# Weights' hi and lo parts kept in DRAM by the first block, and a recurrence's transfers on GpSimd's queue

## The chip, the cores and the metric

One core of one Trainium2 chip runs the kernel. The metric is the device time of an execution in microseconds; the lower is the better.

## The reference

It is one layer of a decoder trunk over 16 meta tokens and a sequence of 2048, with 1024 channels, in float32:

```python
u = rms_norm(h, norm_mix_g)
proj = u @ w_in + b_in
y_attn = sliding_window_sink_attention(q, k, v, sinks)
y_rwkv = rwkv7_time_mix(p_rwkv, ...)
merged = gates[..., :D] * (y_attn @ w_br_attn) + gates[..., D:] * (y_rwkv @ w_br_rwkv)
h = h + merged @ w_o
f = rms_norm(h, norm_ffn_g)
h = h + (silu(f @ w_ffn_gate) * (f @ w_ffn_up)) @ w_ffn_down
return rms_norm(h, norm_final_g)[:, 16:]
```

The attention looks back 128 positions in 8 heads (2 for keys and values) with rotary positions and a sink. The other mixer is RWKV-7, a recurrence with a state of 64x64 for each of 8 heads. The products of weights are a 1024 x 4640 input projection, two of 512 x 1024, one of 1024 x 1024, and three of 1024 x 2816.

## The kernel before, in words

**Precision.** A product with a weight is made of three matmuls on TensorE in the type fp32r: hi times hi, hi times lo and lo times hi, where hi is the rounded value and lo what rounding leaves. `mm3` (line 221) emits the three. Weights and activations are both split so.

**Weights.** They come in chunks of 128 x 1024 floats (512 KB). A chunk is eight weight tiles of 128 x 128. `chunk` (line 208) loads one into `wraw` (two buffers) on SP's queue, writes the hi part with ACT and the lo part with DVE into tiles of the tag `wsp` (five buffers, so two chunks and a half). All this has high priority: the framework's planner, which fixes each engine's order of instructions from a simulated timeline, puts it as early as buffers allow. Each of the four blocks loads and splits the same 119 chunks again: 37 of `w_in`, 8 of `w_br`, 8 of `w_o`, 22 each of gate, up and down.

**Blocks and phases.** The sequence is cut into four blocks of 512 positions. First `phase_a` (line 353) runs for all four blocks: norm, input projection, and its outputs to DRAM (`proj_d`, `gate_d`). Then `phase_c` (line 440) runs for all four: branch products, gates, output projection, FFN, final norm. `add_to_h` (line 377) adds the products of `w_o` and `w_down` to the residual.

**Mixers.** Attention (`attn`, line 914, 16 tiles of 128 positions) and recurrence (`rwkv`, line 606, 32 units of 256 positions and one pair of heads, and one unit for the meta tokens) are generators. The driver (line 1060 on) advances them by `tick` while the phases emit dense work, a step for some microseconds of it. TensorE's instructions run in the order in which they are emitted (`InOrder`, whose calls all have line 93); the queues of the other engines are ordered by the planner and then run strictly in order.

**One unit of the recurrence.** After its elementwise work on ACT and DVE, a product `g` is made (line 739). Four transfers on SP write it to `lt_d` in DRAM (line 744), one reads it back as `lt`, spread over the partitions (line 754), and one loads the start value `xv` (line 757); `xv` and `lt` have one buffer each. GpSimd then inverts triangular blocks in 31 steps of a product `pr` and a sum into `xv` (lines 761, 763) and writes the result to `xt_d` on its own queue (line 788). Some ticks later four transfers on SP read it as `td` (line 793; one buffer, which the unit before still reads until its last step). DVE transposes a part of it into `tq` (line 797), TensorE forms `pq` from that, and the four steps of the recurrence follow: `ch` on TensorE, copies `rd`, `sf`, `yt` on ACT, `ud` and the state `sd` on DVE. The output's norm has a power on GpSimd (line 850), and `yf` goes to `y_d` on SP (line 861), from where `phase_c` loads it (`Ys`, line 405).

**What else is on GpSimd:** the rotary positions of attention (`q`, `kl`, `kr`, lines 883 to 885 and 934 to 936), the power in each norm (line 232), a part of the final scaling (line 526).

**What else is on SP:** the loads of x, of the projections for the mixers, of y and the gates, and a part of the output. A line 202 in the rows is any call of high priority on ACT or DVE, 212 is the load of a weight.

Of the kernel before, what the change touches and what calls it, by code (L numbers as in the profile page):

```python
# [19 lines left out]
F32 = mybir.dt.float32  # L20
# [7 lines left out]
P = 128  # L28
# [50 lines left out]
def layer(ctx, tc, x, meta, w_in, w_br, w_o, w_gate, w_up, w_down, w2a, a2, g2, vecs, sinks, gfin,  # L79
# [124 lines left out]

    HA, HV = High(A), High(V)


    def chunk(src, name, pin=False):

        with tc.high_priority():  # L210
            raw = dn.tile([P, D], F32, tag="wraw", bufs=2, name=f"wr_{name}")
            r = S.dma_start(raw, src)
            if name == "in_0_%d" % ORDER[0]:
                late(r)
        hi, lo = (dn.tile([P, D], F32R, tag="wsp", bufs=5, name=f"w{q}_{name}") for q in "hl")
        made = HA.activation(hi, raw, AF.Copy), HV.tensor_sub(lo, raw, f32(hi))
        if pin:
            late(made[0]), late(made[1])
        return hi, lo

# [132 lines left out]
    def phase_a(b):  # L353
        u = nxt[0] or rows_of(b)
        nxt[0] = None
        rest = None
        ws = []
        mid = lambda ci: lambda: ws.append(chunk(w_in[ci], f"in_{b}_{ci}", True))
        for n_, ci in enumerate(ORDER):
            w = ws.pop(0) if ws else chunk(w_in[ci], f"in_{b}_{ci}")  # L360
            if ci == ORDER[20] and b < NB - 1:
                nxt[0] = rows_of(b + 1)
            if ci == ORDER[-1] and b == NB - 1:
                nxt[0] = Ys(0)
            yield from in_chunk(b, ci, u, w, nxt[0] if ci == ORDER[-1] else None, mid(ORDER[n_ + 1]) if b == 0 and n_ < 2 else None)
            if rest:
                rest()
                rest = None
            if b == 0 and ci == ORDER[0]:
                load_rest()  # L370
                meta_norm()
            if b == 0 and ci in META_CH:
                rest = meta_chunk(ci, w)
            else:
                emitted[b].add(ci)

    def add_to_h(h, ms, src, name, last=None):

# [3 lines left out]
        def part(t, hf):  # L382
            if hf not in ws:
                ws[hf] = chunk(src[hf], f"{name}_{hf}")
            w = ws[hf]
# [54 lines left out]
    def phase_c(b):  # L440
# [6 lines left out]
        for f in range(KT):  # L447
            tg = []
            for q in range(2):
                g_ = dn.tile([P, 512], F32, tag="ld", bufs=4, name=f"tg_{b}_{f}_{q}")  # L450
                S.dma_start(g_, gate_d[8 * q + f][:, tk])
                tg.append(g_)
            w = chunk(w_br[f], f"br_{b}_{f}")
            y[0]
# [14 lines left out]
            if len(grp) == 4:  # L469
                yield from add_to_h(h, grp[:2], w_o[f // 2 - 1], f"o{b}_{f}")  # L470
                grp = grp[2:]
        rows, st = [], []

        def normed(t, hf):
# [3 lines left out]
            if hf:  # L478
# [8 lines left out]

        yield from add_to_h(h, grp, w_o[KT // 2 - 1], f"o{b}_l", normed)
        grp = []
        yield NORM_US  # L490
        fz = Acts(rows, "g_ffn", f"f{b}")
        ws = [chunk(w_gate[0], f"g_{b}_0")]

        mids = [lambda: ws.append(chunk(w_up[0], f"u_{b}_0", True)),
                lambda: ws.append(chunk(w_gate[1], f"g_{b}_1", True))]
        for n in range(NFF):
            pss = []
            for nm, src in (("g", w_gate), ("u", w_up)):
                w = ws.pop(0) if ws else chunk(src[n], f"{nm}_{b}_{n}")
                ps = psd.tile([P, 512], F32, tag="pd", name=f"p{nm}_{b}_{n}")  # L500
                yield from product(ps, w, fz, mid=mids.pop(0) if mids else None)
                pss.append(ps)
            th = dn.tile([P, 512], F32, tag="tmp", bufs=2, name=f"th_{b}_{n}")
            HA.activation(th, pss[0], AF.Tanh, scale=0.5)
            HV.scalar_tensor_tensor(th, th, 1.0, pss[0], op0=ALU.add, op1=ALU.mult)
            HV.tensor_mul(th, th, pss[1])
            grp.append(split_of(th, f"g{b}_{n}"))
            if len(grp) == 4:
                yield from add_to_h(h, grp[:2], w_down[n // 2 - 1], f"d{b}_{n}")
                grp = grp[2:]  # L510
# [19 lines left out]

        yield from add_to_h(h, grp, w_down[NFF // 2 - 1], f"d{b}_l", finished)

# [73 lines left out]
    def rwkv(i, j):  # L606
# [125 lines left out]
        for x in range(2):  # L732
# [5 lines left out]
            if x == 0:  # L738
                V.tensor_mul(g[:, :, 0], pv[:, :, 0], rnb.unsqueeze(2).to_broadcast([P, n, CH]))
                for h in range(2):  # L740
                    for q in range(2):
                        r32, o = slice(64 * h + 32 * q, 64 * h + 32 * q + 32), slice(32 * q, 32 * q + 32)
                        m0 = (2 * q + h) * 4
                        S.dma_start(lt_d[uid, m0:m0 + n].rearrange("c j i -> j c i"), g[r32, :, 0, o])
                V.tensor_mul(g[:, :, 1], pv[:, :, 1], cc("gincl").unsqueeze(1).to_broadcast([P, n, CH]))
            else:
# [6 lines left out]
        lt = mx.tile([P, 32, 32], F32, tag="lt", bufs=1, name=f"lt_{nm}")  # L753
        S.dma_start(lt.rearrange("p j i -> p (j i)"),
                    lt_d[uid].rearrange("m j i -> m (j i)").unsqueeze(0).to_broadcast([8, 16, 1024]))
        xv = mx.tile([P, 4, 32], F32, tag="xv", bufs=1, name=f"xv_{nm}")
        S.dma_start(xv.rearrange("p c i -> p (c i)"), consts[:, slice(*_CC["x0"])])
        for r in range(31):
# [31 lines left out]
        for h in range(2):  # L790
            for q, r32 in ((0, lo[h]), (1, hi[h])):
                m0 = (2 * q + h) * 4
                S.dma_start(td[r32, :, r32], xt_d[uid, m0:m0 + 4].rearrange("m j i -> j m i"))
        yield
# [65 lines left out]
        V.tensor_mul(yf, yf, gs)  # L860
        S.dma_start(y_d[4 + j][:, i * TU:(i + 1) * TU], yf)

# [315 lines left out]
```

## Time and profile before

| what | value |
|---|---|
| median of 3 runs | 3419.69 us (3419.29 to 3424.39) |
| the profiled execution | 3412.06 us |
| its span, first to last instruction | 3410.3 us |
| TensorE, matmuls | 3263.3 us busy, 96% |
| DVE | 1929.6 us, 57% |
| ACT | 1499.4 us, 44% |
| GpSimd (POOL) | 1004.8 us, 29% |
| mean granted TensorE clock | 0.984 |
| DMA | 409.50 MB, 120 GB/s on average |

PE is TensorE's matmuls, PEld its loads of weights into the array, which run beside them. Busy time counts instructions of the engine; time in which it waits or issues a transfer is not busy, but on GpSimd the issue of a transfer is listed as work. A row of waits says which instruction sat idle, what ended the wait, and how long this was in total, how often, and at most. A row of the timeline is: start, duration, engine, line, operation, output and inputs, and in brackets the idle time before it with what ended it. The granted clock is 1.00 at 2.4 GHz and 0.50 at 1.2 GHz.

### The profile page before, as it was taken

How to read it: one execution, taken by the hardware profiler on the slowest of the kernel's cores; microseconds unless marked ns; L12 is line 12 of the kernel's file. 1: busy time of each engine (PE TensorE's matmuls, PEld its weight loads, DVE VectorE, ACT ScalarE, POOL GpSimd, SP SyncE). 2: the span in 40 equal slices, each digit the busy share in tenths (PEclk: the TensorE clock that was granted, in tenths of full speed). 3: DMA queues.
4: the chain of work that ended last, by engine and by line, in shares of the span. 5: the costliest groups of instructions: out<-in, count | busy, mean ns of one | idle time of the engine just before them, and what ended most of it. 6: DMA issues, size and time to landing. Idle time of an engine off the chain costs nothing.

```text
span 3410.3 us, 47506 instructions
## 1 busy us (share of the span) xinstructions
PE 3263.3 (96%) x16909; PEld 2682.7 (79%) x16909; DVE 1929.6 (57%) x3860; ACT 1499.4 (44%) x3101; POOL 1004.8 (29%) x2290
## 2 busy tenths in 40 slices
PE   8999999999999989999989899999989999999999
PEld 6887778887778777778868788887777888778887
DVE  3344445554544775656667656657655555764455
ACT  4455456554544564445443533434353333432222
POOL 0133333343333343333343244334333341100000
PEclk9999999999999999999989999999999999999999
DMA  4544444454544433333244333335332332522222
GB/s 144 160 144 129 161 133 134 140 157 133 163 131 139 142 103 103 97 91 102 85 139 151 95 102 101 90 98 168 122 95 85 102 94 90 196 96 94 98 99 99
DMA packets 227027, 409.50 MB, mean 120 GB/s; under 512 B 61829, under 2 KB 120581, under 8 KB 226790
## 3 DMA queue, kind: packets, MB, share of 16 engines
q1 hardware_dynamic: 192854, 356.98, 34.5%
q10 hardware_dynamic: 32352, 47.31, 4.0%
q8 instruction: 133, 2.18, 0.3%
q0 software_dynamic: 1584, 2.18, 0.2%
q14 instruction: 104, 0.85, 0.1%
HBM read 346.29 MB, written 60.04 MB: 119 GB/s over the span
## 4 chain that ended last, share of the span: by engine, by line
PE 46%; issue 20%; POOL 20%; DMA 7%; DVE 4%; ACT 2%; SPq 1%; POOLq 0%; ACTq 0%; DVEq 0%
PE pi L93 15%; POOL pr L761 9%; POOL xv L763 8%; PE pg L93 7%; PE pu L93 7%; PE ph_d L93 5%; PE ch L93 2%; PE pb L93 1%; PE ph_o L93 1%; PE py L93 1%; DMA lt<-lt_d 1%; DMA wr_in<-in_w_in 1%; DMA xt_d<-xv 1%; DVE h L202 1%; PE ph_d_l L93 1%
## 5 line engine op out<-in xcount | busy, mean ns | idle before, releaser
L93 PE MATMUL pi<-act_u,wh_in 128*128 128x512 f32 x2368 | 764.1, 404 | 2.3 <-DVE act_u L202 2.1
L761 POOL TENSOR_TENSOR pr<-xv,lt 128x124 f32<-128x124 f32 (+30 forms) x992 | 398.1, 401 | 584.6 <-DMA lt<-lt_d 468.9
L93 PEld LDWEIGHTS pi<-act_u,wh_in 128*128 128x128 f32 x2368 | 425.3, 190 | 83.2 <-issue 5.7
L93 PE MATMUL pi<-act_u,wl_in 128*128 128x512 f32 x1184 | 465.6, 393 | 0.6 <-DVE wl_in L202 0.6
L93 PE MATMUL pg<-act_f,wh_g 128*128 128x512 f32 x1408 | 453.6, 403 | 7.2 <-DVE act_f L202 7.1
L93 PE MATMUL pu<-act_f,wh_u 128*128 128x512 f32 x1408 | 446.7, 398 | 0.0
L93 PE MATMUL ph_d<-wh_d,mg_g 128*128 128x512 f32 x1280 | 428.4, 399 | 16.4 <-DVE th L202 13.6
L763 POOL TENSOR_TENSOR xv<-xv,pr 128x124 f32<-128x124 f32 (+30 forms) x992 | 380.9, 384 | 76.5
L93 PEld LDWEIGHTS pg<-act_f,wh_g 128*128 128x128 f32 x1408 | 256.5, 190 | 57.5 <-DVE act_f L202 9.8
L93 PEld LDWEIGHTS pu<-act_f,wh_u 128*128 128x128 f32 x1408 | 257.5, 189 | 50.3 <-issue 1.5
L93 PEld LDWEIGHTS ph_d<-wh_d,mg_g 128*128 128x128 f32 x1280 | 241.7, 189 | 69.8 <-DVE th L202 15.2
L202 DVE TENSOR_TENSOR wl_in<-wr_in,wh_in 128x1024 fp32r<-128x1024 f32 x148 | 187.0, 1264 | 184.4 <-PE pi L93 126.8
L93 PE MATMUL pg<-act_f,wl_g 128*128 128x512 f32 x704 | 277.6, 394 | 0.0
L93 PE MATMUL pu<-act_f,wl_u 128*128 128x512 f32 x704 | 275.8, 392 | 0.0
L93 PEld LDWEIGHTS pi<-act_u,wl_in 128*128 128x128 f32 x1184 | 223.4, 189 | 51.0 <-DVE wl_in L202 1.0
L93 PE MATMUL ph_d<-wl_d,mg_g 128*128 128x512 f32 x640 | 250.4, 391 | 0.0
L850 POOL TENSOR_TENSOR gst<-gst,mhalf 128x4 f32<-128x4 f32 x32 | 36.1, 1128 | 707.2 <-DVE gst L849 656.8
L202 DVE SCALAR_TENSOR_TENSOR h<-ph_d,h 128x512 f32<-128x512 f32 x320 | 216.5, 685 | 49.1 <-PE ph_d L93 48.1
L202 ACT ACTIVATE wh_g<-wr_g 128x1024 fp32r<-128x1024 f32 x88 | 93.3, 1060 | 220.3 <-PE ph_d L93 81.5
L202 ACT ACTIVATE wh_in<-wr_in 128x1024 fp32r<-128x1024 f32 x148 | 155.8, 1053 | 56.1 <-DMA wr_in<-in_w_in 47.5
L202 DVE TENSOR_TENSOR wl_d<-wr_d,wh_d 128x1024 fp32r<-128x1024 f32 x80 | 99.3, 1242 | 133.1 <-PE pg L93 53.6
L202 DVE TENSOR_TENSOR wl_u<-wr_u,wh_u 128x1024 fp32r<-128x1024 f32 x88 | 108.4, 1232 | 115.5 <-issue 54.2
(358 smaller groups left out, 5940.3 us busy)
## 6 DMA issues: line engine op xcount, KB each, us to landing
wr_in<-in_w_in SPq DMA_DIRECT2D x148, 512.0 KB, 3.8
wr_g<-in_w_gate SPq DMA_DIRECT2D x88, 512.0 KB, 3.6
wr_u<-in_w_up SPq DMA_DIRECT2D x88, 512.0 KB, 3.4
wr_d<-in_w_down SPq DMA_DIRECT2D x80, 512.0 KB, 3.3
proj_d<-po ACTq DMA_DIRECT2D x84, 256.0 KB, 2.5
gate_d<-po ACTq DMA_DIRECT2D x64, 256.0 KB, 2.2
lt<-lt_d SPq DMA_DIRECT2D x32, 512.0 KB
wr_br<-in_w_br SPq DMA_DIRECT2D x32, 512.0 KB, 5.1
```

The source lines that it names most:

```text
L93: r = f(*p, **k)
L202: return f(*p, **k)
L761: G.tensor_mul(pr[:, :, :n_], xv[:, :, r:r + 1].to_broadcast([P, 4, n_]), lt[:, r, r + 1:].unsqueeze(1).to_broadcast([P, 4, n_]))
L763: G.tensor_add(xv[:, :, r + 1:], xv[:, :, r + 1:], pr[:, :, :n_])
L850: G.tensor_tensor(st[:, 3], st[:, 2], mhalf[:, 0:4], op=ALU.pow)
```

## The change

`chunk` gets a key that names the weight. The first block to ask for a key loads the raw weight in two halves of 128 x 512 (`wraw`, two buffers of half the size), splits each half on ACT and DVE into one tile that holds both parts (`wsp`, three buffers of both parts, 1 MB each), and writes that tile to a new DRAM tensor on GpSimd's queue. The other three blocks load that tensor, 1 MB in one transfer on SP's queue, and neither ACT nor DVE touches it. `w_in` is made in the first `phase_a`, all other weights in the first `phase_c`. In the recurrence, the transfers for `lt_d`, `lt`, `xv`, `td` and `y_d` are issued by GpSimd instead of SP. Nothing else differs. The callers pass the key: `("in", ci)`, `("br", f)`, `("o", f // 2 - 1)` and a half, `(nm, n)` for gate and up, `("d", n // 2 - 1)` and a half.

```diff
@@ -202,21 +202,32 @@
                     return f(*p, **k)
             return g
 
-    HA, HV = High(A), High(V)
-
-
-    def chunk(src, name, pin=False):
-
-        with tc.high_priority():
-            raw = dn.tile([P, D], F32, tag="wraw", bufs=2, name=f"wr_{name}")
-            r = S.dma_start(raw, src)
-            if name == "in_0_%d" % ORDER[0]:
-                late(r)
-        hi, lo = (dn.tile([P, D], F32R, tag="wsp", bufs=5, name=f"w{q}_{name}") for q in "hl")
-        made = HA.activation(hi, raw, AF.Copy), HV.tensor_sub(lo, raw, f32(hi))
-        if pin:
-            late(made[0]), late(made[1])
-        return hi, lo
+    HA, HV, HG = High(A), High(V), High(G)
+
+
+    parts_d = {}
+
+    def chunk(src, name, key, pin=False):
+
+
+        w = dn.tile([P, 2, D], F32R, tag="wsp", bufs=3, name=f"w_{name}")
+        if key in parts_d:
+            with tc.high_priority():
+                S.dma_start(f32(w.rearrange("p q c -> p (q c)")), parts_d[key])
+            return w[:, 0], w[:, 1]
+        for hf in range(2):
+            c = slice(hf * 512, (hf + 1) * 512)
+            with tc.high_priority():
+                raw = dn.tile([P, 512], F32, tag="wraw", bufs=2, name=f"wr_{name}_{hf}")
+                r = S.dma_start(raw, src[:, c])
+                if name == "in_0_%d" % ORDER[0]:
+                    late(r)
+            made = HA.activation(w[:, 0, c], raw, AF.Copy), HV.tensor_sub(w[:, 1, c], raw, f32(w[:, 0, c]))
+            if pin:
+                late(made[0]), late(made[1])
+        parts_d[key] = dp.tile([P, 2 * D], F32, name=f"wd_{name}")
+        HG.dma_start(parts_d[key], f32(w.rearrange("p q c -> p (q c)")))
+        return w[:, 0], w[:, 1]
 
     def mm3(ps, lh, ll, rh, rl, start, stop):
         T.matmul(ps, lh, rh, start=start, stop=False)
...
@@ phase_a @@
-        mid = lambda ci: lambda: ws.append(chunk(w_in[ci], f"in_{b}_{ci}", True))
+        mid = lambda ci: lambda: ws.append(chunk(w_in[ci], f"in_{b}_{ci}", ("in", ci), True))
-            w = ws.pop(0) if ws else chunk(w_in[ci], f"in_{b}_{ci}")
+            w = ws.pop(0) if ws else chunk(w_in[ci], f"in_{b}_{ci}", ("in", ci))
...
@@ -741,7 +752,7 @@
                     for q in range(2):
                         r32, o = slice(64 * h + 32 * q, 64 * h + 32 * q + 32), slice(32 * q, 32 * q + 32)
                         m0 = (2 * q + h) * 4
-                        S.dma_start(lt_d[uid, m0:m0 + n].rearrange("c j i -> j c i"), g[r32, :, 0, o])
+                        G.dma_start(lt_d[uid, m0:m0 + n].rearrange("c j i -> j c i"), g[r32, :, 0, o])
                 V.tensor_mul(g[:, :, 1], pv[:, :, 1], cc("gincl").unsqueeze(1).to_broadcast([P, n, CH]))
             else:
                 V.tensor_mul(g.rearrange("p c q t -> p c (q t)"), pg.rearrange("p (c f) -> p c f", f=P),
...
@@ -751,10 +762,10 @@
         lt = mx.tile([P, 32, 32], F32, tag="lt", bufs=1, name=f"lt_{nm}")
-        S.dma_start(lt.rearrange("p j i -> p (j i)"),
+        G.dma_start(lt.rearrange("p j i -> p (j i)"),
                     lt_d[uid].rearrange("m j i -> m (j i)").unsqueeze(0).to_broadcast([8, 16, 1024]))
         xv = mx.tile([P, 4, 32], F32, tag="xv", bufs=1, name=f"xv_{nm}")
-        S.dma_start(xv.rearrange("p c i -> p (c i)"), consts[:, slice(*_CC["x0"])])
+        G.dma_start(xv.rearrange("p c i -> p (c i)"), consts[:, slice(*_CC["x0"])])
         for r in range(31):
             n_ = 31 - r
             pr = mx.tile([P, 4, 32], F32, tag="pr", bufs=1, name=f"pr_{nm}_{r}")
...
@@ -790,7 +801,7 @@
         for h in range(2):
             for q, r32 in ((0, lo[h]), (1, hi[h])):
                 m0 = (2 * q + h) * 4
-                S.dma_start(td[r32, :, r32], xt_d[uid, m0:m0 + 4].rearrange("m j i -> j m i"))
+                G.dma_start(td[r32, :, r32], xt_d[uid, m0:m0 + 4].rearrange("m j i -> j m i"))
         yield
         tq = mx.tile([P, n, 32], F32, tag="tl", bufs=2, name=f"tq_{nm}")
         for h in range(2):
...
@@ -858,7 +869,7 @@
         A.activation(yf, pyt[:, :TU], AF.Identity, bias=vc("ln_b", j), scale=vc("ln_w", j))
         V.tensor_add(yf, yf, bv)
         V.tensor_mul(yf, yf, gs)
-        S.dma_start(y_d[4 + j][:, i * TU:(i + 1) * TU], yf)
+        G.dma_start(y_d[4 + j][:, i * TU:(i + 1) * TU], yf)
...
```

## Rows read from the trace of the kernel before

**Rows 1.** Busy time of each engine by stage: input blocks 0 and 1 to 3, output blocks 0 to 3

```profile
core 0: us, PE busy (x) PEld busy (x) DVE busy (x) ACT busy (x) POOL busy (x), PEclk, DMA share, GB/s
30.00:270.00 240.00, 238.23 (x1280) 194.29 (x1278) 91.17 (x217) 106.66 (x215) 41.84 (x85) 1.00 0.47 145
280.00:1127.00 847.00, 825.84 (x4434) 675.64 (x4433) 409.19 (x963) 444.31 (x991) 311.70 (x707) 0.99 0.47 143
1130.00:1770.00 640.00, 601.67 (x3166) 490.39 (x3165) 412.03 (x893) 300.36 (x678) 235.11 (x536) 0.97 0.35 104
1775.00:2360.00 585.00, 559.68 (x2984) 464.41 (x2982) 372.20 (x715) 245.14 (x503) 215.82 (x519) 0.98 0.37 111
2370.00:2955.00 585.00, 558.85 (x2915) 464.36 (x2914) 362.09 (x672) 231.38 (x462) 174.04 (x400) 0.98 0.36 111
2960.00:3390.00 430.00, 424.99 (x1876) 350.63 (x1875) 228.31 (x297) 123.48 (x155) 2.17 (x4) 0.99 0.31 103
```

**Rows 2.** Waits of PE: us in total, times, longest us

```profile
PE py L93 <- ACT ptt L991: 15.6, 6, 5.1
PE ph_d L93 <- DVE th L202: 13.6, 5, 10.4
PE pt_f L93 <- DVE f L202: 11.6, 4, 8.8
```

**Rows 3.** Waits of SP's own queue, not those of the weights

```profile
SPq L757 <- DMA xt_d<-xv: 341.5, 30, 17.1
...
SPq L744 <- DVE g L745: 123.0, 32, 11.2
SPq L793 <- PE ch L93: 103.6, 25, 9.3
```

**Rows 4.** Timeline of SP, ACT and PE from 2615 to 2622

```profile
2615.65 0.33 SPq L757 DMA_DIRECT2D xv<-in_consts  x1
2616.08 0.38 SPq L212 DMA_DIRECT2D wr_g<-in_w_gate  x1
...
2619.70 1.06 ACT L202 ACTIVATE wh_g<-wr_g 128x1024 fp32r<-128x1024 f32 x1 [13.38 <-DMA wr_g<-in_w_gate]
...
2621.10 0.80 PE L93 MATMUL ch<-vd,g 128*128 128x128 f32 x2 [4.93 <-ACT yt L836]
```

**Rows 5.** Busy time around five stalls, first and last of five (columns as in rows 1)

```profile
1160.00:1180.00 20.00, 14.99 (x72) 12.47 (x71) 11.34 (x26) 7.36 (x15) 0.00 (x0) 0.83 0.46 149
...
2612.00:2632.00 20.00, 15.07 (x69) 12.53 (x68) 6.08 (x17) 5.44 (x12) 1.39 (x5) 0.83 0.26 87
```

**Rows 6.** Groups of instructions: the two halves of a weight's split

```profile
L202 DVE TENSOR_TENSOR wl_in<-wr_in,wh_in 128x1024 fp32r<-128x1024 f32 x148 | 187.0, 1264 | 184.4 <-PE pi L93 126.8 <-ACT rd L824 15.6 <-PE pm L93 15.0
...
L202 ACT ACTIVATE wh_in<-wr_in 128x1024 fp32r<-128x1024 f32 x148 | 155.8, 1053 | 56.1 <-DMA wr_in<-in_w_in 47.5 <-PE pm L93 8.1 <-ACT po L202 0.5
```

**Rows 7.** What touches tile xv on GpSimd: duration ns min/median/max

```profile
L761 POOL TENSOR_TENSOR pr<-xv,lt x992: 202/321/1426, 301.7 to 2831.7; 128x124 f32<-128x124 f32 x7, 128x104 f32<-128x104 f32 x7, 128x84 f32<-128x84 f32 x7, 128x64 f32<-128x64 f32 x7
...
L788 POOL DMA_DIRECT2D xt_d<-xv x32: 652/680/687, 336.7 to 2832.5; - x32
```

**Rows 8.** Groups of instructions: the inversion's product, busy us, mean ns, and its waits

```profile
L761 POOL TENSOR_TENSOR pr<-xv,lt 128x124 f32<-128x124 f32 (+30 forms) x992 | 398.1, 401 | 584.6 <-DMA lt<-lt_d 468.9 <-DMA kr<-proj_d 41.9
```

**Rows 9.** Timeline of GpSimd and DVE at 717.6

```profile
717.59 1.47 POOL L763 TENSOR_TENSOR xv<-xv,pr 128x120 f32<-128x120 f32 x1
...
717.57 1.22 DVE L202 TENSOR_TENSOR wl_in<-wr_in,wh_in 128x1024 fp32r<-128x1024 f32 x1
```

**Rows 10.** Timeline of DVE and PE from 2232 to 2239

```profile
2232.75 0.62 DVE L797 STREAM_TRANSPOSE tq<-td 32x128 f32<-32x128 f32 x2
...
2238.53 0.59 PE L93 MATMUL pq<-tq,g 32*32 32x32 f32 x16
```

**Rows 11.** Timeline of ACT at 1501.7

```profile
1501.71 1.29 ACT L873 ACTIVATE kw<-kl 64x128 fp32r<-64x128 f32 x4 [11.21 <-POOL kl L885]
```

**Rows 12.** DMA issues: KB each, median us from issue to landing

```profile
wr_in<-in_w_in SPq DMA_DIRECT2D x148, 512.0 KB, 3.8
...
xt_d<-xv POOLq DMA_DIRECT2D x32, 64.0 KB, 2.3
```

More of the change, by code (lines that the diff above doesn't have):

```diff
@@ L375, in phase_a, with add_to_h @@
                 emitted[b].add(ci)
-    def add_to_h(h, ms, src, name, last=None):
+    def add_to_h(h, ms, src, name, key, last=None):
         ws = {}
@@ L383, in part @@
             if hf not in ws:
-                ws[hf] = chunk(src[hf], f"{name}_{hf}")
+                ws[hf] = chunk(src[hf], f"{name}_{hf}", key + (hf,))
             w = ws[hf]
@@ L452, in phase_c @@
                 tg.append(g_)
-            w = chunk(w_br[f], f"br_{b}_{f}")
+            w = chunk(w_br[f], f"br_{b}_{f}", ("br", f))
             y[0]
@@ L469, in phase_c @@
             if len(grp) == 4:
-                yield from add_to_h(h, grp[:2], w_o[f // 2 - 1], f"o{b}_{f}")
+                yield from add_to_h(h, grp[:2], w_o[f // 2 - 1], f"o{b}_{f}", ("o", f // 2 - 1))
                 grp = grp[2:]
@@ L486, in normed @@
                 HA.activation(rows[t][1], h[:, t, 512:], AF.Copy, scale=r)
-        yield from add_to_h(h, grp, w_o[KT // 2 - 1], f"o{b}_l", normed)
+        yield from add_to_h(h, grp, w_o[KT // 2 - 1], f"o{b}_l", ("o", KT // 2 - 1), normed)
         grp = []
@@ L491, in phase_c @@
         fz = Acts(rows, "g_ffn", f"f{b}")
-        ws = [chunk(w_gate[0], f"g_{b}_0")]
-        mids = [lambda: ws.append(chunk(w_up[0], f"u_{b}_0", True)),
-                lambda: ws.append(chunk(w_gate[1], f"g_{b}_1", True))]
+        ws = [chunk(w_gate[0], f"g_{b}_0", ("g", 0))]
+        mids = [lambda: ws.append(chunk(w_up[0], f"u_{b}_0", ("u", 0), True)),
+                lambda: ws.append(chunk(w_gate[1], f"g_{b}_1", ("g", 1), True))]
         for n in range(NFF):
@@ L498, in phase_c @@
             for nm, src in (("g", w_gate), ("u", w_up)):
-                w = ws.pop(0) if ws else chunk(src[n], f"{nm}_{b}_{n}")
+                w = ws.pop(0) if ws else chunk(src[n], f"{nm}_{b}_{n}", (nm, n))
                 ps = psd.tile([P, 512], F32, tag="pd", name=f"p{nm}_{b}_{n}")
@@ L508, in phase_c @@
             if len(grp) == 4:
-                yield from add_to_h(h, grp[:2], w_down[n // 2 - 1], f"d{b}_{n}")
+                yield from add_to_h(h, grp[:2], w_down[n // 2 - 1], f"d{b}_{n}", ("d", n // 2 - 1))
                 grp = grp[2:]
@@ L529, in finished @@
                     e.dma_start(out[b * TB + t * P:b * TB + (t + 1) * P, c], h[:, t, c])
-        yield from add_to_h(h, grp, w_down[NFF // 2 - 1], f"d{b}_l", finished)
+        yield from add_to_h(h, grp, w_down[NFF // 2 - 1], f"d{b}_l", ("d", NFF // 2 - 1), finished)
     sd = [cp.tile([P, P], F32, name=f"sd{j}") for j in range(4)]
```

## The prediction

> **What bounds the kernel now.** I read the stages first, then who TensorE waits for, then SP's own queue, and last the stretches where the waits fall. In the table by stage TensorE is busy nearly all the time: six stretches that hold 3327 us of the span leave it idle for 1.8 us in the first input block, 21.2 in the other three, 38.3, 25.3 and 26.2 in the first three output blocks and 5.0 in the last [rows 1]. Their sum, 117.8 us, is about all that any change beside TensorE's work can win, with what the clock loses after the longer stalls. None of its waits of over 1 us names a DMA or a weight's part; what ends its idle time is ACT or DVE, late with something small, up to 10.4 us [rows 2].
>
> Why those are late is seen in SP's queue. SP issues in program order, and its longest wait outside the weights is line 757: the start value xv of the next inversion may be loaded only when the last one has been written out by GpSimd, 341.5 us in 30 waits [rows 3]. One case in full: xv is let go at 2615.65, wr_g, queued behind it, goes out at 2616.08, ACT had stood 13.38 us at the split of wr_g with the recurrence's copy yt behind it, and TensorE idled 4.93 us for yt [rows 4]. The same chain (xv, then a load of weights or of y, then ACT) ends at 1167.5, 1749.7, 1850.3, 2455.7 and 2621.1: five stalls.
>
> **The change, part by part.**
>
> *Transfers off SP.* In the five 20 us stretches around those stalls TensorE is idle for 27.6 us, and the granted clock averages 0.79 (first and last stand in [rows 5]), so the lower level of 1.2 GHz held for 2 x 0.206 x 100 = 41 us; at least 41 - 27.6 = 13.6 us of that was work, which costs half, 6.8 us. Together 34 us; from below 0, if the loads are late for another reason, from above 27.6 + 20.6 = 48. I take **-34**, since the xv wait leaves SP entirely. What is late next is the load's own landing. The Trainium skill (DMA: Bandwidth & Descriptors, Issuing engines are not separate DMA queues) says that spreading issue over engines saves only issue time, which is small. Here it is the order of waits that costs, and by the rule the -34 would be 0.
>
> *Splits gone from blocks 1 to 3.* A block has 119 chunks (37 w_in, 8 w_br, 8 w_o, 66 of the FFN). 357 pairs of ACT 1.053 us and DVE 1.264 us go [rows 6]: 376 and 451 us of the 1044 and 1372 us that these engines are busy in those blocks [rows 1], about a third. None of it is on TensorE's path by itself; what shrinks is the wait of others behind it. The idle time of these blocks is 77.7 us; 12.9 of it are three of the five stalls (3.1, 4.9 and 4.9), and some 19 are held by GpSimd (below, 27 less 8 in the first output block). A third of the other 46: **-15**, bounds 0 and -46.
>
> *GpSimd.* Its queue takes 11 transfers for each of 32 units and 10 for the meta unit, 362, and 119 writes of parts, at 0.68 us an issue [rows 7]: 246 + 81 us. On the other side, pr has a median of 321 ns but a maximum of 1426 [rows 7] and a mean of 401 over 992 [rows 8]; with sizes that fall evenly mean and median should agree, so 79 us of pr are stalls, and I take as much for xv, whose steps alternate with it. The long ones lie beside DVE's subtractions for wl, as the step of 1.47 us here [rows 9], and those go in three blocks. Net at most +327 and at least +169 us of GpSimd.
>
> The recurrence's path: lt_d's four issues take 2.7 us instead of 1.75 and the rest perhaps 1 us more; the chain is some 4 us shorter where the splits are gone. td's four loads come about 1.5 us later, and DVE's transposes with them, but TensorE reaches the product that reads them 5.2 us after their end [rows 10]. Cost **0**; without that cover 32 x 1.5 = 48 us.
>
> What is queued behind the new waits on GpSimd is the attention's rotary work, the norms' powers and the final scaling. Their lateness is in the trace already: ACT stood 11.21 us for kl [rows 11], and TensorE's waits py (15.6) and pt_f (11.6) [rows 2], 27 us, end on such steps. GpSimd is now busy or held by lt for 981 + 469 us of the six stretches [rows 1, 8]; added are 169 us and the waits that move: 123.0 for g, 103.6 for td's readers [rows 3], and 33 landings of xt_d at 2.3 us [rows 12], 303 in all. 1450 becomes 1922, a third more: **+9**, bounds 0 and +48 (the cover above).
>
> The Trainium skill (the same page, SWDGE vs HWDGE vs iDMA) warns that GpSimd writes its descriptors into SBUF, and that VectorE in its two-port mode locks it out there. The trace has 32 such issues between 0.652 and 0.687 us [rows 7], none held up, and I add nothing for it; by the rule each could grow as pr does.
>
> *Block 0.* Raw weights now come in halves through two half-size buffers, ACT and DVE pay two starts for a chunk, and 1 MB of parts is written for each. A half's landing lies between 2.3 us (64 KB) and 3.8 (512 KB) [rows 12]; with 3 us, an issue of 0.4 [rows 4], and some 0.6 and 0.7 for the halves of the split, a buffer turns in 4.7 us, so two give a chunk every 4.7 us. TensorE uses one every 7.8 us in the first output block (640 us for 82) and every 6.5 to 7.6 in the first input block (240 to 280 for 37; I take 7.0) [rows 1]. That covers it, except where the recurrence leaves stretches as dense as the last block, 430/82 = 5.2 us. DMA is the thin spot: 145 GB/s at a share of 0.47 [rows 1]; 1 MB more each 7.0 us is 150 GB/s, a share of 0.95. I take **+5**, bounds 0 and +119 (1 us a chunk).
>
> *Blocks 1 to 3, loads.* Each chunk is now one load of 1 MB, and three buffers let it start two chunks ahead: 10.4 us in the densest stretch. 512 KB land in 3.8 us [rows 12]; twice that is 7.6 with nothing else in the queue. SP's other waits can eat the rest now and then: **+4**, bounds 0 and +36 (0.1 us for each of 357).
>
> Sum: -34 - 15 + 9 + 5 + 4 = -31. The profiled execution took 3412.06 us (span 3410.3), so it would take 3381; the median of the runs shown lies 7.6 us above it, so **3389 us**.
>
> **The rivals.**
>
> *A larger gain.* All that ACT and DVE hold in blocks 1 to 3 goes (-46), and the clock's loss is at its upper bound (-48), with GpSimd's +9: -85, 3335 us. For it: both engines lose a third of their work. Against: many of the waits are short chains of dependent steps, not queues. Chance 0.10.
>
> *No change.* By the skill's rule above, an issue queue is worth only its issue time. As a mechanism here: the five stalls re-form, because a load that leaves earlier lands later, being twice as large, and the norms and the recurrence are chains of dependent steps. Then -34 and -15 fall away, and so do the small losses: 3420 us. Against it, the 13 us that ACT stood are SP's time, not the load's [rows 4]. Chance 0.12.
>
> *Slower: block 0's ring.* The mechanism is the two half buffers with the writes beside them. If a half's landing rises so that a buffer turns in more than 7.0 us in the first input block, or 5.2 in dense stretches of the first output block, each of its 119 chunks comes late, and ACT, in order, stands at the split and holds the recurrence's copies. At 0.5 us a chunk it costs 60 us instead of 5: 3389 + 55 = 3444. It decides from 0.3 us a chunk on. For it: a DMA share near 0.95 and writes that queue behind GpSimd's waits, which keep the buffer. Against: three part buffers smooth it, and on average the turn is covered. Chance 0.26.
>
> That the change doesn't do what it says can't be the case for the splits, whose instructions simply aren't there in three blocks.
>
> **How the numbers follow.** The forecast has 0.52, from 3352 to 3410. About 0.2% (7 us) is what a measurement of this kernel can tell from no change. Faster: 0.52 + 0.10 = 0.62; same 0.12; slower 0.26. The range runs from 3340, which leaves out half of the larger gain, to 3440, which leaves out about half of the slower case.
>
> **What would show it.** Right: no wait of SP on xt_d; TensorE's stalls at the five places gone, and idle time in blocks 1 to 3 near 55 us; pr's maximum rare outside block 0; GpSimd busy for some 1200 us; TensorE's rows naming a load of weights for under 5 us. Wrong: idle time in the first blocks above 60 us with ACT waiting for a raw half or for a write of parts (the slower case); rows of TensorE waiting for loads of 1 MB; py and pt_f waits well above 36 us, with GpSimd standing at a transfer.

## The result, and the profile after

| | before | after |
|---|---|---|
| median | 3420.83 us (3419.29 to 3424.39, 4 runs) | 3376.03 us (3366.40 to 3377.94, 4 runs) |
| profiled execution | 3412.06 us | 3377.94 us |
| its span | 3410.3 us | 3376.0 us |
| mean granted clock | 0.984 | 0.987 |

The ratio is 0.9862, with an interval from 0.9841 to 0.9882: the changed kernel is faster by 1.4%, some 45 us. The forecast was 3389 us, with 3340 to 3440 as its range. The total held; below it will be seen that two of its terms were wrong by about the same amount in opposite directions.

The page of the kernel after: busy time, the slices of DMA load, and the DMA queues (packets, MB, share of 16 engines).

```profile
PE 3256.3 (96%) x16909; PEld 2681.2 (79%) x16909; DVE 1542.1 (46%) x3622; ACT 1163.2 (34%) x2863; POOL 1156.1 (34%) x2771
...
DMA  7777666676666776666668555556755555855555
GB/s 262 273 261 241 209 226 211 190 227 197 223 210 215 242 260 206 234 235 234 231 237 280 176 170 174 179 181 201 263 171 177 171 177 176 288 179 191 196 191 181
DMA packets 229448, 721.46 MB, mean 214 GB/s; under 512 B 36333, under 2 KB 90989, under 8 KB 168286
...
q1 hardware_dynamic: 158126, 516.15, 47.1%
q0 software_dynamic: 38736, 154.99, 12.9%
```

ACT lost 336 us of work and DVE 388, GpSimd gained 151; the bytes rose from 409.50 to 721.46 MB. The stage table of the kernel after, in the stretches of [rows 1] without the last, in which the kernel now ends. The blocks have shifted by up to 37 us against these stretches, so the work in them is nearly, not exactly, the same:

```profile
core 0: us, PE busy (x) PEld busy (x) DVE busy (x) ACT busy (x) POOL busy (x), PEclk, DMA share, GB/s
30.00:270.00 240.00, 222.11 (x1167) 180.31 (x1167) 87.53 (x223) 102.53 (x225) 53.05 (x97) 0.96 0.79 276
280.00:1127.00 847.00, 823.02 (x4403) 674.09 (x4402) 270.08 (x848) 342.67 (x874) 324.93 (x814) 0.99 0.66 212
1130.00:1770.00 640.00, 611.50 (x3228) 498.65 (x3227) 426.97 (x979) 313.98 (x774) 326.52 (x703) 0.98 0.69 236
1775.00:2360.00 585.00, 571.79 (x3075) 477.31 (x3074) 298.86 (x670) 175.89 (x456) 236.44 (x611) 0.99 0.60 194
2370.00:2955.00 585.00, 575.65 (x3013) 479.78 (x3012) 280.83 (x601) 146.74 (x374) 181.36 (x468) 0.99 0.60 201
```

In the first input block TensorE is now idle for 17.9 us of 240, where it was 1.8, and the DMA share there went from 0.47 to 0.79. The first output block improved from 38.3 to 28.5 us idle, the next two from 25.3 and 26.2 to 13.2 and 9.4; input blocks 1 to 3 went from 21.2 to 24.0. So the gain lies in the output blocks, and the first input block pays.

The waits of the kernel after, TensorE's first, then SP's and GpSimd's (us in total, times, longest us). Lines of the recurrence and of attention are 11 higher than before: 768 is the load of xv, 772 the step pr.

```profile
PE psS L93 <- DVE qs L956: 27.3, 9, 5.8
...
PE pt_f L93 <- DVE f L202: 5.6, 6, 1.5
PE py L93 <- ACT ptt L1002: 4.8, 2, 3.3
...
PE pb L93 <- DMA w_br<-wd_br: 0.6, 1, 0.6
...
SPq L216 <- PE pi L93: 460.1, 82, 11.9
...
POOL td L804 <- PE ch L93: 197.3, 25, 17.7
...
POOL pr L772 <- DMA lt<-lt_d: 176.8, 32, 13.5
...
POOL xv L768 <- DMA xt_d<-xv: 92.4, 28, 6.2
```

SP has no wait on xt_d any more, which was its longest outside the weights [rows 3]; GpSimd stands there instead, for 92.4 us rather than 341.5, and waits for lt 176.8 us rather than 468.9 [rows 8]. SP now waits for TensorE to let go of a weight's tile (line 216). py and pt_f fell from 27 us to 10.4 [rows 2]; the longest row is now psS, the scores of attention, waiting for qs, which hangs on the rotary steps of GpSimd. Only one row of TensorE names a load, with 0.6 us. What touches xv, in the kernel after (duration in ns, min/median/max):

```profile
L772 POOL TENSOR_TENSOR pr<-xv,lt x992: 197/317/937, 328.3 to 2798.1; 128x124 f32<-128x124 f32 x7, 128x104 f32<-128x104 f32 x7, 128x84 f32<-128x84 f32 x7, 128x64 f32<-128x64 f32 x7
...
L768 POOL DMA_DIRECT2D xv<-in_consts x32: 554/563/622, 289.2 to 2731.6; - x32
```

The mean of pr fell from 401 [rows 8] to 333 ns, near its median. An issue of xv on GpSimd's queue costs 0.56 us, where the prediction took 0.68 for every issue.

### The profile page after: what moved, and what is told of

It reads as the page before. It is cut to its first block, busy times and chain, and to the rows that moved or that the text cites. A ratio compares the mean times of both kernels' runs of the same rounds, so it can differ in the third digit from the quotient of the medians.

```text
span 3376.0 us, 47237 instructions
## 1 busy us (share of the span) xinstructions
PE 3256.3 (96%) x16909; PEld 2681.2 (79%) x16909; DVE 1542.1 (46%) x3622; ACT 1163.2 (34%) x2863; POOL 1156.1 (34%) x2771
## 2 busy tenths in 40 slices
DMA packets 229448, 721.46 MB, mean 214 GB/s; under 512 B 36333, under 2 KB 90989, under 8 KB 168286
## 4 chain that ended last, share of the span: by engine, by line
PE 60%; DMA 6%; DVE 3%; POOL 3%; ACT 2%; issue 2%; SPq 0%; POOLq 0%; DVEq 0%; ACTq 0%
PE pg L93 14%; PE pu L93 12%; PE ph_d L93 11%; PE pi L93 6%; PE pb L93 4%; PE ch L93 4%; PE ph_o L93 3%; DMA yl<-y_d 1%; PE ph_o_l L93 1%; POOL pr L772 1%; POOL xv L774 1%; DMA lt<-lt_d 1%; PE py L93 1%; PE pq L93 1%; DVE h L202 1%
## 5 line engine op out<-in xcount | busy, mean ns | idle before, releaser
L93 PE MATMUL pi<-act_u,w_in 128*128 128x512 f32 x3552 | 902.5, 402 | 10.5 <-DVE m L202 6.1
L93 PEld LDWEIGHTS pi<-act_u,w_in 128*128 128x128 f32 x3552 | 652.9, 191 | 144.0 <-issue 5.5
L93 PE MATMUL pg<-act_f,w_g 128*128 128x512 f32 x2112 | 533.7, 399 | 6.8 <-DVE act_f L202 6.8
L93 PE MATMUL pu<-act_f,w_u 128*128 128x512 f32 x2112 | 522.9, 395 | 0.0
L93 PE MATMUL ph_d<-w_d,mg_g 128*128 128x512 f32 x1920 | 472.5, 397 | 10.4 <-DVE h L202 10.0
L93 PEld LDWEIGHTS pg<-act_f,w_g 128*128 128x128 f32 x2112 | 388.4, 189 | 85.3 <-DVE act_f L202 9.0
L93 PEld LDWEIGHTS pu<-act_f,w_u 128*128 128x128 f32 x2112 | 388.9, 188 | 78.8 <-issue 1.0
L93 PEld LDWEIGHTS ph_d<-w_d,mg_g 128*128 128x128 f32 x1920 | 355.5, 189 | 85.9 <-DVE h L202 14.5
L772 POOL TENSOR_TENSOR pr<-xv,lt 128x124 f32<-128x124 f32 (+30 forms) x992 | 330.5, 333 | 248.9 <-DMA lt<-lt_d 176.8
L93 PE MATMUL pb<-ya,w_br 128*128 128x512 f32 x768 | 191.0, 400 | 1.0 <-DMA w_br<-wd_br 0.6
L93 PE MATMUL ph_o<-w_o,mg_m 128*128 128x512 f32 x576 | 144.2, 400 | 6.8 <-DVE h L202 3.8
L202 ACT ACTIVATE th<-pg 128x512 f32<-128x512 f32 x88 | 52.6, 598 | 281.4 <-PE pg L93 281.0
```

Of the source, the lines that this page charges most:

```text
L93: r = f(*p, **k)
L202: return f(*p, **k)
L772: G.tensor_mul(pr[:, :, :n_], xv[:, :, r:r + 1].to_broadcast([P, 4, n_]), lt[:, r, r + 1:].unsqueeze(1).to_broadcast([P, 4, n_]))
```

## The experiments

**The two parts of the change, each alone.** The first kernel is the changed one with the five transfers put back on SP; the second is the kernel before with the five on GpSimd (`S.dma_start` becomes `G.dma_start` at lines 744, 754, 757, 793 and 861), and nothing else; the third moves line 757 alone:

```diff
-        S.dma_start(xv.rearrange("p c i -> p (c i)"), consts[:, slice(*_CC["x0"])])
+        G.dma_start(xv.rearrange("p c i -> p (c i)"), consts[:, slice(*_CC["x0"])])
```

The fourth is the changed kernel with nothing kept: halves are loaded and split in every block, nothing is written.

```diff
-        parts_d[key] = dp.tile([P, 2 * D], F32, name=f"wd_{name}")
-        HG.dma_start(parts_d[key], f32(w.rearrange("p q c -> p (q c)")))
```

Weights alone:

> The parts are kept in DRAM as in the changed kernel, but the recurrence's five kinds of transfers go back to SP. Theory A (SP's order is what cost: the wait for xv holds the loads behind it): the xv wait stands again ahead of the loads of weights, now ahead of loads of 1 MB that TensorE reads directly; at most a third of the 45 us is left, 3406 to 3440 us, and TensorE's rows name loads of weights. Theory B (the splits gone from ACT and DVE are the gain, the queue is worth only issue time): 3375 to 3390 us, with no such rows.

Transfers alone:

> The kernel before with the five kinds of transfers on GpSimd and nothing else. Theory A: the five stalls behind xv go, GpSimd's chain is not shortened (the splits are all there): 34 us less, 9 to 15 us given back on GpSimd, 3395 to 3402 us. Theory B: no change, 3414 to 3428 us.

The load of xv alone:

> The kernel before with the load of xv alone on GpSimd. Theory A: this one wait was the harm, so it gains as much as all five kinds moved, or somewhat more as GpSimd takes fewer waits: 3385 to 3400 us. If the other waits of SP (lt_d for g, td for ch, y_d) do the same harm, it gains less than half of what moving all five gains. Theory B: no change.

Nothing kept:

> The changed kernel without keeping anything: every block loads halves and splits them, no writes of parts, the transfers on GpSimd. It shows the ring of two half buffers alone. If the ring is what cost 20 us in the first input block (the slower case of the prediction), each of the 476 chunks is exposed to it, the first input block stays near 281 us and the time is above 3440. If it is the writes (traffic, or GpSimd held by them), the first input block is back at 261 to 266 us and the time is that of the transfers alone, within 10 us.

| kernel | median us | ratio to before | interval |
|---|---|---|---|
| kept weights alone | 3417.55 | 0.9992 | 0.9975 to 1.0008 |
| five transfers alone | 3339.41 | 0.9751 | 0.9731 to 0.9772 |
| xv's load alone | 3357.00 | 0.9805 | 0.9783 to 0.9826 |
| nothing kept (transfers, halves) | 3350.93 | 0.9783 | 0.9766 to 0.9800 |
| the change | 3376.03 | 0.9862 | 0.9841 to 0.9882 |

The transfers alone bring 80 us, one load of 64 KB 62 of them. Both beat their forecasts by far (3395 to 3402 and 3385 to 3400 us), which had been built on the same five stalls as the prediction. Keeping the weights brings nothing alone, and on top of the transfers it loses 37 us (3376 against 3339). Half buffers without keeping cost 11.5 by the medians, but the two intervals overlap. The changed kernel is faster than before because of a line that has nothing to do with weights.

Where this happens is seen by block. The table has the length in us of each block, from its first product to the next block's first; the values of seven kernels come from stage tables cut there. The last three columns are experiments that follow.

| block | before | five transfers | nothing kept | the change | writes, unused | small writes | xv on SP, two buffers, pinned |
|---|---|---|---|---|---|---|---|
| input 0 | 260.6 | 257.0 | 259.0 | 281.0 | 280.9 | 262.0 | 260.0 |
| input 1 | 289.3 | 287.3 | 286.4 | 288.6 | 284.7 | 287.1 | 287.8 |
| input 2 | 276.6 | 278.8 | 277.8 | 289.9 | 279.7 | 289.4 | 277.5 |
| input 3 | 284.3 | 276.6 | 281.1 | 274.6 | 279.6 | 273.2 | 284.8 |
| output 0 | 648.7 | 623.7 | 624.9 | 640.9 | 643.0 | 624.8 | 616.2 |
| output 1 | 592.1 | 575.9 | 574.5 | 568.3 | 576.6 | 564.9 | 579.0 |
| output 2 | 574.7 | 554.7 | 553.0 | 546.0 | 550.9 | 546.2 | 549.7 |
| output 3 | 467.9 | 469.5 | 473.1 | 470.4 | 471.0 | 468.7 | 468.6 |

The transfers win in output blocks 0 to 2, 25.0 + 16.2 + 20.0 = 61 us. Keeping the weights (the change against nothing kept) loses 22 us in input block 0 and 16 in output block 0, the two in which parts are written, and 8 in input blocks 1 to 3; it wins 16 in output blocks 1 to 3.

**What in the writes costs.** GpSimd's queue stands at each write until DVE has made the lo part, and the write moves 1 MB beside the other loads. One kernel lets ACT issue the writes, so that GpSimd isn't held; one does not keep w_in, so that nothing is written in the input blocks; one keeps every wait of GpSimd, but writes an eighth of the bytes.

```diff
-        HG.dma_start(parts_d[key], f32(w.rearrange("p q c -> p (q c)")))
+        HA.dma_start(parts_d[key], f32(w.rearrange("p q c -> p (q c)")))
```

> The changed kernel with one difference: the 119 writes of parts to DRAM are issued by ACT instead of GpSimd. Bytes moved stay the same. Where does the price of keeping the parts (3376 us against 3339 with the transfers alone; most of it in the first input block, 281 against 257 us, and the first output block, 641 against 624) come from? Theory (GpSimd is held: a write waits on its queue for DVE's lo part, up to 11.9 us, while the attention's rotary steps stand behind it): the first input block falls from 281 to about 260 us, the kernel to about 3350. Rival (traffic: 1 MB more per chunk, a DMA share of 0.78 there, makes the loads that the mixers wait for late): the first input block stays near 281 us, the kernel at 3370 to 3380. Second rival (ACT is worse placed, since TensorE's copies stand behind its writes): 3390 us or more.

```diff
+        if key[0] == "in":
+            return w[:, 0], w[:, 1]
         parts_d[key] = dp.tile([P, 2 * D], F32, name=f"wd_{name}")
```

> The changed kernel, but the parts of w_in are not kept: they are split in every input block, and only the other 82 weights are written in the first output block and loaded ready-made in the other three. If what keeping w_in costs is all in the input blocks (1134 us against 1104 without any keeping), and the output blocks are as in the changed kernel: 3376 - 30 = about 3346 us, first input block near 259 us. If the first input block's loss comes from something else in the change: no less than 3365 us, and that block stays near 280 us.

```diff
+            small = dp.tile([P, 2, D // 8], F32, name=f"wd_{name}")
+            HG.dma_start(small, f32(w[:, :, :D // 8]))
...
+        parts_d[key] = parts_d[0]
```

> The changed kernel with every write of parts but the first cut to one eighth of its bytes (128 KB of 1 MB), issued and waited for by GpSimd at the same place; the later blocks load 1 MB for each chunk, all from the one tensor that is written whole, so the weights of most products are not the reference's. If the cost is GpSimd held at the write's wait for DVE: first input block stays near 281 us, kernel 3370 to 3380 us. If it is the traffic of the writes: first input block near 260 us, first output block near 625, kernel about 3340 us.

Measured: writes on ACT 3396.41 us (0.9930, 0.9903 to 0.9956); w_in not kept 3352.60 us (0.9809, 0.9781 to 0.9838); small writes 3334.98 us (0.9753, 0.9732 to 0.9773). With ACT as the issuer the first input block stays at 282.3 us, so GpSimd being held was not it, and the first output block grows to 661.6, so that the total lies where the second rival had put it. With an eighth of the bytes, and the same waits of GpSimd, both blocks come back to 262.0 and 624.8. Without w_in's writes the first input block is 259.6, while the first output block, with its writes, stays at 647.6. It is the traffic. A write could also hold up the work by keeping its tile, but in the kernel after no wait of ACT or DVE ends on a write of parts.

That kernel with small writes also loads all its parts from one tensor, so one more was run in which nothing but the writes differs from the kernel with nothing kept: the first block writes its parts and nobody reads them.

```diff
-        if key in parts_d:
-            with tc.high_priority():
-                S.dma_start(f32(w.rearrange("p q c -> p (q c)")), parts_d[key])
-            return w[:, 0], w[:, 1]
...
+        if key not in parts_d:
+            parts_d[key] = dp.tile([P, 2 * D], F32, name=f"wd_{name}")
+            HG.dma_start(parts_d[key], f32(w.rearrange("p q c -> p (q c)")))
```

> The changed kernel without the loads of ready-made parts: every block loads raw halves and splits them, and the first block writes its parts to DRAM on GpSimd's queue, where nobody reads them. It stands between the kernel with nothing kept (3351 us) and the changed kernel (3376 us). If the writes of 1 MB a chunk beside the other loads are the cost: first input block near 281 us, first output block near 641, the others as with nothing kept, together about 3351 + 40 = 3390 us. If the loss in the first blocks came from the planner's other order or from a buffer rather than from the writes: near 3355 us, first input block near 260.

It took 3389.21 us (0.9915, 0.9899 to 0.9932), as expected. This makes a ladder of medians: before 3419.4, transfers 3339.4 (**-80**), half buffers 3350.9 (**+11.5**), writes 3389.2 (**+38**), parts loaded ready-made 3376.0 (**-13**). The intervals of the ratios are some 7 us wide to each side, so each step is known no better than that. By the ratios, each taken against the kernel before that ran beside it, the writes cost 45 us and the ready-made parts bring 18; between the two profiled executions the last step is 7 us (spans of 3382.8 and 3376.0).

How traffic reaches TensorE is seen in the DMA issues of the first input block (KB each, median us from issue to landing); the kernel after:

```profile
DMA packets 33721, 76.55 MB, mean 272 GB/s; under 512 B 7768, under 2 KB 13912, under 8 KB 28770
...
wd_in<-w_in POOLq DMA_DIRECT2D x36, 1024.0 KB, 5.9
wr_in<-in_w_in SPq DMA_DIRECT2D x70, 256.0 KB, 4.0
...
kr<-proj_d SPq DMA_DIRECT2D x8, 16.0 KB, 3.9
```

The same block with nothing kept:

```profile
DMA packets 28792, 37.25 MB, mean 144 GB/s; under 512 B 7234, under 2 KB 13378, under 8 KB 28771
...
wr_in<-in_w_in SPq DMA_DIRECT2D x76, 256.0 KB, 3.0
...
kr<-proj_d SPq DMA_DIRECT2D x8, 16.0 KB, 1.7
```

Twice the bytes make a half of a weight land in 4.0 us instead of 3.0, and a load of 16 KB for attention in 3.9 instead of 1.7. With unused writes, which differ from nothing kept in the writes alone, the two take 3.8 and 3.9 us, and with small writes 3.3 and 1.8. One case in the kernel after, from the timeline (start, duration, engine, line, operation, and in brackets the idle time before it with what ended it):

```profile
134.04 1.39 SPq L901 DMA_DIRECT2D kr<-proj_d  x3
...
136.42 1.29 SPq L942 DMA_DIRECT2D vl<-proj_d  x1
...
140.89 0.45 POOL L895 TENSOR_TENSOR kr<-kr,cs 128x128 f32<-128x128 f32 x1 [6.53 <-DMA vl<-proj_d]
...
141.90 1.30 ACT L884 ACTIVATE kw<-kl 64x128 fp32r<-64x128 f32 x4 [3.41 <-POOL kl L896]
...
142.59 1.20 PE L93 MATMUL psS<-kw,qs 128*128 128x144 f32 x4 [7.11 <-ACT kw L884]
```

The last of attention's loads of k is issued by 135.4. The view of tile kr has 5.6 us to landing here as the median, so it lands near 140.7, about when the load of v does, which the row names. GpSimd starts the rotary step at 140.89, ACT follows at 141.90, and TensorE, whose instructions run in the order written, has stood 7.11 us at the scores. No weight is awaited in this chain. They are late too, mostly beside it: ACT's waits for raw halves in this block, kernel after:

```profile
ACT w_in L202 <- DMA wr_in<-in_w_in: 33.7, 24, 5.5
```

and with nothing kept:

```profile
ACT w_in L202 <- DMA wr_in<-in_w_in: 6.9, 7, 3.1
```

TensorE's own waits in this block tell the two apart, kernel after:

```profile
PE psS L93 <- ACT kw L884: 7.1, 1, 7.1
PE pi L93 <- DVE m L202: 6.1, 3, 3.8
PE psS L93 <- DVE qs L956: 4.7, 1, 4.7
```

and with nothing kept:

```profile
PE pi L93 <- DVE m L202: 1.3, 2, 0.8
PE psS L93 <- DVE qs L954: 0.3, 1, 0.3
```

Attention's scores (psS) account for 11.8 us. The row of pi is the smaller part: in its longest case, 3.8 us ending at 40.4, DVE's copy m stood behind two splits, and ACT had waited 2.15 us for their raw halves. So late weights do reach TensorE, by way of DVE's order. In the first output block psS waits for qs 7.6 us, with nothing kept 1.1.

Input block 2 shows the price of the ready-made loads. There the change takes 289.9 us and the kernel with unused writes 279.7. SP's first wait in that block, kernel after:

```profile
SPq L216 <- PE pi L93: 172.9, 29, 11.9
```

and with unused writes:

```profile
SPq L218 <- DVE w_in L202: 108.3, 54, 7.1
SPq L218 <- DMA wr_in<-in_w_in: 51.2, 25, 7.0
```

A ready-made part goes straight into the tile that TensorE still reads, so SP stands at it until TensorE is done, with attention's loads behind it. TensorE's waits in that block are psS for qs, two in 11.5 us. The loads also land later there: qr of attention, 64 KB, after 5.7 us instead of 2.9. Which of the two it is, SP's stand or the extra bytes, wasn't tried.

**Why one load of 64 KB is worth 62 us.** Theory: SP issues in order and stands at the wait for xt_d, and everything behind is late. Rival: GpSimd's queue serves xv better. The test keeps every transfer on SP and takes away what makes it wait, with a second buffer (its room comes from a setup tile).

```diff
-        xv = mx.tile([P, 4, 32], F32, tag="xv", bufs=1, name=f"xv_{nm}")
+        xv = mx.tile([P, 4, 32], F32, tag="xv", bufs=2, name=f"xv_{nm}")
```

> The kernel before with xv in two buffers instead of one (the room comes from a setup tile that is only used at the start); every transfer stays on SP's queue. The load of a unit's xv then waits for the write of the unit before the last, which is long done. If what cost 62 us was SP standing in order at that wait (theory): about 3357 us, as with xv's load alone on GpSimd. If it was something else that GpSimd's queue does better (its issue, or xv's load next to the steps that read it): little changes, 3400 us or more. Between the two, say 3375: part of it is xv's own lateness on a queue whose next waits take its place.

It took 3418.94 us (1.0001, 0.9989 to 1.0013): nothing. By its numbers that speaks for the rival, but SP's waits in this kernel show that the edit hadn't done what it was for:

```profile
SPq L757 <- DMA xt_d<-xv: 318.5, 29, 17.1
```

The planner used the free buffer to issue the load one unit earlier, as soon as its simulated time let it: the first unit's load goes out at 172.1 us, with one buffer it did at 257.0. SP stood at the same writes as before. So the load was also pinned behind what stands before it in the program, the load of its own lt:

```diff
-        S.dma_start(xv.rearrange("p c i -> p (c i)"), consts[:, slice(*_CC["x0"])])
+        late(S.dma_start(xv.rearrange("p c i -> p (c i)"), consts[:, slice(*_CC["x0"])]))
```

> As with xv in two buffers (3419 us, where SP still stood 318.5 us at that load, since the planner, with a buffer more, issues it one unit earlier and so waits for the same write), and the load is now pinned on SP behind the load of lt of its own unit. At that place the write that it waits for is a whole unit old. Theory (what cost 62 us is SP standing in order at that wait, wherever the load is issued): SP's wait for xt_d falls from 318.5 us to under 30, and the kernel to about 3357 us, as with xv's load on GpSimd; up to 3375 if part of the wait goes over to the load of lt. Rival (SP's stand is not the cause, GpSimd's queue serves xv better): the wait goes, and the time stays at 3400 us or more.

It took 3349.54 us (0.9782, 0.9761 to 0.9803), with all five transfers on SP. The view of line 757 in this kernel has no waiting for a semaphore left, only the loads:

```profile
L757 SPq DMA_DIRECT2D xv<-in_consts x32: 417/452/459, 295.1 to 2726.0; - x32
...
DMA to landing us min/median/max: 6.8/7.9/8.1
```

Whose queue it is matters little here (3357.0 on GpSimd, 3349.5 on SP); that nobody stands in line behind the wait does. The Trainium skill (DMA: Bandwidth & Descriptors, Issuing engines are not separate DMA queues) says that issue from several engines saves only issue time. This pair agrees with it as far as the transfer goes, SP serves xv as well as GpSimd; the wait that an instruction carries is another matter, and it was worth 75 us.

Sums of the stage tables cut by block, before and with the pinned load (first the length of all blocks, then busy time by engine):

```profile
sum 3394.20, PE 3259.66 PEld 2680.46 DVE 1923.94 ACT 1486.96 POOL 998.42; mean PE 407.46 PEld 335.06 DVE 240.49 ACT 185.87 POOL 124.80
```

```profile
sum 3323.60, PE 3239.92 PEld 2667.29 DVE 1921.61 ACT 1487.18 POOL 999.03; mean PE 404.99 PEld 333.41 DVE 240.20 ACT 185.90 POOL 124.88
```

The blocks are 70.6 us shorter: TensorE is busy for 19.7 us less with the same matmuls, while the mean granted clock went from 0.984 to 0.991, and idle for 83.7 instead of 134.5, so 50.9 less. DVE, ACT and GpSimd are as busy as before. The middle of the chain shows in ACT, which waited 242 us for raw weights before and 110 now. One row of TensorE's waits, before and with the pinned load, holds 18.1 of the 50.9 us, the largest part in one row:

```profile
PE ch L93 <- ACT yt L836: 23.0, 12, 4.9
```

```profile
PE ch L93 <- ACT yt L836: 4.9, 4, 4.0
```

The next largest drop is that of ph_d waiting for th, 13.6 us [rows 2] and now 2.2; the rest is spread over many rows.

**A faster version.** If order on SP's queue costs, attention's loads (lines 890, 921, 924, 928, 931) might gain as well. Weights are split in every block as before; the second kernel puts xv back on SP, with two buffers and pinned.

> The kernel before with the recurrence's five transfers on GpSimd (3339 us) and, beside them, the attention's loads of its angles, q, k and v, 96 more transfers, on GpSimd too. If order on SP's queue still costs (SP waits there for rotary buffers that GpSimd and ACT free): about 3325 us, faster than any kernel so far. If SP's other waits lie beside the loads' lead and cost nothing: 3335 to 3343 us. If GpSimd's own queue becomes the bound (issues of 0.6 us and waits ahead of the recurrence's steps): 3350 us or more.

> The fastest kernel so far (recurrence's transfers and attention's loads on GpSimd, no parts kept, 3329 us), with xv's load put back on SP, in two buffers and pinned behind SP's last instruction of the program before it. If GpSimd's stand at xv's load (66.5 us in 28 waits) was worth something: 3318 to 3326 us. If that stand lay beside the landing of lt, which ends later: 3327 to 3331. If SP is delayed anew: 3335 or more.

The first took 3329.08 us (0.9734, 0.9713 to 0.9755), the lowest of all and 47 us below the change. Beside the five transfers alone (0.9751, 0.9731 to 0.9772) the intervals overlap, so the second step is likely and not certain; most of it lies in the first output block, 614.5 us against 623.7. (The trace has 196 transfers that moved, not the 96 of the expectation.) The second took 3331.69 us; its ratio is 0.9780 (0.9763 to 0.9796) because the kernel before ran in 3406.24 us beside it, where it took 3417 to 3425 beside the others. Nothing was won by it.

## Why the prediction was right, and where it was not

The time came out right for a sum of which two terms were wrong: the transfers brought 46 us more than forecast, and writes and half buffers cost some 45 more. That the two nearly cancel is luck.

*Transfers off SP: -34, bounds 0 and -48; measured -80, with what GpSimd pays for them.* The mechanism was right: the wait for xv on SP, and what queues behind it. The size failed at the step "in the five 20 us stretches around those stalls TensorE is idle for 27.6 us", taken as all that the wait costs. Those were the stalls long enough to be picked out one by one. Removing the wait took away 50.9 us of idle time and 19.7 us of busy time at a lower clock, 70.6 in all, so what it did outside those five stretches weighs about as much as the 34 us taken for them, and the upper bound, built from the same five, was none. A bound could have been had from [rows 1]: the idle time of output blocks 0 to 2, 89.8 us.

*Splits gone: -15, and loads +4; measured -13 together.* This is the step from unused writes to the change, -7 between the profiled executions. By blocks it is plainer: 14 us won in output blocks 1 to 3, 9 lost in input blocks 1 to 3. With the transfers still on SP it was worth more, kept weights alone made output block 2 shorter by 31 us (574.7 to 543.6), as if there both terms drew on the same stalls.

*GpSimd: +9, not seen as a loss.* The change added 151 us of work to it, less than the forecast's least, 169, which took each issue too dear. GpSimd has 1208 us of work with the five transfers alone, 203 more than before, as issues at 0.56 us make it; py and pt_f fell to 11.7 us there. Against xv fixed on SP (3349.5) the five transfers on GpSimd are, if anything, faster (3339.4).

*Block 0: +5, bounds 0 and +119; measured +38 for the writes.* The step that failed is "that covers it": it asked only whether weights arrive in time. The share of 0.95 was feared, it became 0.79; but already there the loads of 16 KB that attention waits for land more than twice as late, and those have no buffer ahead of them. The rival for this case had the place right, the price in part (38 us over 119 chunks are 0.32 us each, about the point from which it was to decide, where it reckoned with 0.5), and a part of the mechanism: ACT did stand at raw halves, but in the first input block TensorE waited 11.8 us at attention's scores and 6.1 us at pi, of which 3.8 behind late splits. The half buffers by themselves add 11.5 us by the medians and 7.2 between the profiled executions: input blocks 0 and 3 and output block 3 are longer by 2.0 to 4.5 us, the others nearly as before. The cause stays open.

*Loads of blocks 1 to 3: +4.* No load of 1 MB is awaited (0.6 us). What they cost, 9 us in input blocks 1 to 3 against the kernel with unused writes, seems to come from SP standing at them or from other loads landing later beside them.

Of the listed signs these came true: no wait of SP on xt_d, pr's long steps gone, GpSimd near 1200 us (1156), loads of weights under 5 us, and idle time of 46.5 us in blocks 1 to 3 without the last, near 50 with it. The first blocks' 46.4 us stayed under the 60 set for the slower case, and yet most of the 38 us is there. A sign that only looks for the mechanism in mind misses its neighbour.

## What to carry to other kernels

A queue that issues in order charges a wait to everything behind it. So rank a queue's waits by their sum, bound the gain by all idle time of the stages where they fall, not by the stalls that one can pick out; and fix it by moving or pinning the one instruction that carries the wait, checking in the trace that the wait is gone, since a planner may spend a new buffer on issuing earlier. Bytes added beside an engine-bound stage are not free because their own consumer is covered: look at which small loads, issued just before they are needed, share the DMA engines. Here, made once and read three times, 1 MB per chunk cost some 38 us to write and brought some 13.

## What the runs showed of the hardware

A load of 64 KB issued right behind one of 512 KB on the same queue lands after 7.9 us, where it took 1.9 before. Its reader needs both and waits 520.3 us in all for the last one, where it waited 468.9, and the kernel is faster all the same.

GpSimd's steps pr and xv, 0.32 us as the median of 2046, took up to 1.5 us in the kernel before. There 142 of them took over 0.9 us, and 139 of these lay beside one of DVE's subtractions of 1.26 us. With the five transfers alone it is 145, with the subtractions in halves of about 0.7 us in every block 7 (the longest 2.1 us), and after the change 2. The mean of all steps falls less: 392, 393, 376 and 340 ns. So halving the subtractions took away the longest stalls but little of their sum; leaving most of them out did.

In the issues of GpSimd there was no sign of DVE holding them up (0.554 to 0.622 us for xv, above).
